# Output projection of a hybrid decoder layer by seven half-size products instead of eight

## The chip, the cores and the metric

The kernel runs on one core of one Trainium2 chip. The metric is the device time of one execution in microseconds (us), as the median of several runs. The engines are called as the profile calls them: PE (TensorE, matrix products; PEld is its weight load), DVE (VectorE), ACT (ScalarE), POOL (GpSimd) and SP (SyncE, which here only issues transfers). Each engine runs its own instructions in a fixed order and waits for the others by semaphores; SP, ACT and POOL each issue transfers in the order of their own instructions.

## What is computed

One decoder layer over 2048 tokens of width 1024, in float32. The change touches the first block's last step, the output projection, and what feeds it:

```python
h = rmsnorm(x, mix_norm_w[i])
proj = h @ w_in[i]
y_s5  = s5_mixer(...)            # diagonal SSM group, 256 columns, ends in y * sigmoid(y @ w_glu)
y_ssd = ssd_mixer(...)           # Mamba-2 group, 768 columns, ends in rmsnorm(y * silu(z), norm_w)
x = x + concatenate([y_s5, y_ssd], -1) @ w_out[i]      # 2048x1024 by 1024x1024
h = rmsnorm(x, xa_norm_w[i])
x = x + cross_attention(h, mem_n, wq, wk, wv, wo)
h = rmsnorm(x, ffn_norm_w[i])
x = x + conv_ffn(h, w_up, conv_w, conv_b, w_down)
return rmsnorm(x, final_norm_w)
```

The rmsnorm inside `ssd_mixer` divides each token's 768 columns by their own root mean square. The 256 columns of `y_s5` are not divided by it.

## The kernel before

Every float32 product is made of three matmuls on split operands: an operand is cut into a rounded high part (ACT, `halves`, L98) and the low rest (DVE, L99), and `mm3` (L123 to L125) adds high by high, high by low and low by high. A matmul has 128 stationary columns and 512 moving ones. So each operand costs one ACT and one DVE instruction per 128x512 tile before PE can take it.

The stages run in this order.

1. **The mixer** (`MixerIn.run`, four blocks of 512 tokens): the input projection, the convolutions, the SSD scan. Its results go to the DRAM tensor `yT`, one 128x1024 row of tiles per 128 tokens, columns 256 to 1023. Generators in the lists `fg`, `bg` and `xg` are advanced a step at a time between the halves of the projections (`Kit.step`). `ssq` makes `rs`, the reciprocal root mean square per token.
2. **The S5 part** (`stage_s5`): its last piece, `glu` (L868 to L876), multiplies gelu by a gate on DVE (L874) and writes columns 0 to 255 of `yT` with a POOL transfer (L875), block by block. Cross-attention's weight products run beside it.
3. **`stage_b`**: the output projection, then the scores, softmax and values of cross-attention. Scores and values already run by seven half-size products (`products`, Strassen-Winograd): two token tiles (a "pair", eight pairs in all) give the four quarters a11, a12, a21, a22 of the left side; `lefts` forms and splits the seven left factors, one per product; `factors` and `right` form and split the seven right factors, 4 tiles of 128x512 per product. `ORDER` (1, 6, 5, 3, 7, 4, 2) is the order of the products.
4. The feed-forward stages `stage_up` and `stage_down`.

In `stage_b` before, the output projection runs tile by tile (16 token tiles, 2 halves of the columns). Per half, `proj` multiplies the six `yT` chunks of the SSD group (p2) and the two of the S5 group (p1) into two PSUM tiles, and DVE adds `rs` * p2 and 0.5 * p1 to x (L1215, L1216). The 16 tiles of `w_out` are split once into the `Q` buffers (7 groups of 8). The first four half-tiles start with the chunks 2, 3, 6 and 7 (`early`), which do not need the S5 part. Towards the end the first right factors of the scores (`Rg`) go into the `Q` groups that are still free, and the left factors of the scores' first pair are made from x1, the result written to DRAM by POOL (L1217).

Raw tiles come through pools: `F` (10 tiles of 128x512), `L` (2 tiles of 128x1024), `X` (6 of 128x1024), `A` (16 left halves). A pool's tile can be loaded again only when its last reader is done.

What stands in which order on an engine is set by the tile scheduler, which orders the program's instructions by priorities and dependences; within an engine nothing overtakes.

## Time and profile before

| what | value |
|---|---|
| time, median of 3 runs | 2668.95 us (2668.3 to 2670.01) |
| time of the profiled execution | 2667.42 us |
| its span | 2665.7 us |
| PE busy | 2603.0 us (98%) |
| DVE busy | 2121.5 us (80%) |
| ACT busy | 1358.0 us (51%) |
| POOL busy | 407.3 us (15%) |
| first and last matmul of `stage_b`'s products | 848.6 and 1367.9 us |
| the output projection, by its first matmul and its last addition to x | 848.6 to 1028.4 us |

Matmuls are pipelined, so the duration of one (389 ns) is longer than the distance between two. The same is true of DVE and ACT instructions: the distance between the starts of two is what a queue costs. Windows and timelines count from the span's start.

### The profile page before, as it was taken

What the parts mean: (1) busy time and instruction counts of PE and PEld (TensorE: products, weight loads), DVE (VectorE), ACT (ScalarE), POOL (GpSimd) and SP (SyncE); (2) the same over time, 40 slices, a digit from 0 to 9 for tenths busy, and PEclk for the clock granted to TensorE, in tenths of its full rate; (3) what the DMA queues carried; (4) which work ended last, traced back from release to release, by engine and by line L of the source; (5) the groups of instructions that cost most, each with busy time, mean ns of one, the idle gap of its engine ahead of it and who ended that gap; (6) DMA issues with size and microseconds to landing.
All of it is one profiled execution on the core that took longest, in us unless ns stands there. A gap on an engine that the chain in (4) does not pass through costs nothing. (4 is left out here: it accounts for less than half of the span.)

```text
span 2665.7 us, 38967 instructions
## 1 busy us (share of the span) xinstructions
PE 2603.0 (98%) x12796; PEld 2150.3 (81%) x12796; DVE 2121.5 (80%) x4034; ACT 1358.0 (51%) x2817; POOL 407.3 (15%) x691
## 2 busy tenths in 40 slices
PE   8999999999999999999999999999999999999998
PEld 6768878788987888888888888888888887788876
DVE  8798898888876537778788878989787877678776
ACT  4655567764556116788554545445444434433333
POOL 1112212111022101202202332212111110000000
PEclk9999999999999999999999999999999999999999
DMA  5565554543586936546762444344222218887886
GB/s 188 173 186 175 182 192 164 164 139 126 177 303 235 336 126 213 182 168 231 261 202 83 128 146 133 103 123 153 80 87 80 87 64 280 278 283 249 262 263 209
DMA packets 244355, 480.94 MB, mean 180 GB/s; under 512 B 30584, under 2 KB 72824, under 8 KB 244152
## 3 DMA queue, kind: packets, MB, share of 16 engines
q1 hardware_dynamic: 182312, 341.38, 38.3%
q0 software_dynamic: 32976, 118.09, 13.8%
q10 hardware_dynamic: 28864, 18.98, 2.3%
q8 instruction: 101, 1.65, 0.3%
q14 instruction: 102, 0.84, 0.1%
HBM read 363.25 MB, written 114.49 MB: 179 GB/s over the span
## 5 line engine op out<-in xcount | busy, mean ns | idle before, releaser
L124 PE MATMUL ps<-H,W 128*128 128x512 f32 x952 | 370.6, 389 | 0.3 <-DVE H L99 0.3
L123 PE MATMUL ps<-H,W 128*128 128x512 f32 x952 | 370.8, 390 | 0.0
L125 PE MATMUL ps<-H,W 128*128 128x512 f32 x952 | 370.4, 389 | 0.0
L123 PE MATMUL ps<-h,w 128*128 128x512 f32 (+1 forms) x736 | 299.1, 406 | 3.1 <-DVE h L102 2.1
L124 PE MATMUL ps<-h,w 128*128 128x512 f32 (+1 forms) x736 | 286.6, 389 | 0.9 <-DVE h L102 0.9
L125 PE MATMUL ps<-h,w 128*128 128x512 f32 (+1 forms) x736 | 286.3, 389 | 0.7 <-DVE w L99 0.7
L123 PE MATMUL ps<-Q,A 128*128 128x512 f32 x704 | 275.8, 392 | 0.8 <-ACT A L98 0.8
L125 PE MATMUL ps<-Q,A 128*128 128x512 f32 x704 | 274.5, 390 | 0.2 <-DVE A L99 0.2
L124 PE MATMUL ps<-Q,A 128*128 128x512 f32 x704 | 273.9, 389 | 0.0
L98 ACT ACTIVATE W<-S 128x512 fp32r<-128x512 f32 x191 | 119.0, 630 | 292.8 <-DVE S L1346 146.1
L98 ACT ACTIVATE w<-r 128x512 fp32r<-128x512 f32 x224 | 139.4, 627 | 139.5 <-PE ps L124 108.7
L124 PEld LDWEIGHTS ps<-H,W 128*128 128x128 f32 x952 | 178.7, 188 | 38.0 <-DVE H L99 1.1
L125 PEld LDWEIGHTS ps<-H,W 128*128 128x128 f32 x952 | 178.7, 188 | 37.2
L123 PEld LDWEIGHTS ps<-H,W 128*128 128x128 f32 x952 | 178.7, 188 | 37.0 <-ACT H L98 0.3
L99 DVE TENSOR_TENSOR w<-r,w 128x512 fp32r<-128x512 f32 x224 | 153.5, 687 | 33.0 <-ACT w L98 31.4
L125 PEld LDWEIGHTS ps<-h,w 128*128 128x128 f32 x736 | 139.4, 189 | 30.6 <-DVE w L99 1.1
L123 PEld LDWEIGHTS ps<-h,w 128*128 128x128 f32 x736 | 139.6, 190 | 29.7 <-DVE h L102 2.3
L124 PEld LDWEIGHTS ps<-h,w 128*128 128x128 f32 x736 | 139.8, 190 | 27.6 <-DVE h L102 2.5
L125 PEld LDWEIGHTS ps<-Q,A 128*128 128x128 f32 x704 | 132.2, 188 | 29.1 <-DVE A L99 1.4
L123 PEld LDWEIGHTS ps<-Q,A 128*128 128x128 f32 x704 | 132.2, 188 | 27.8 <-ACT A L98 1.0
L124 PEld LDWEIGHTS ps<-Q,A 128*128 128x128 f32 x704 | 132.3, 188 | 26.6
L98 ACT ACTIVATE A<-F 128x512 fp32r<-128x512 f32 (+1 forms) x146 | 89.1, 631 | 126.4 <-PE ps L124 74.1
(474 smaller groups left out, 6187.4 us busy)
## 6 DMA issues: line engine op xcount, KB each, us to landing
A<-actd SPq DMA_DIRECT2D x192, 256.0 KB, 3.6
r<-in_w_in SPq DMA_DIRECT2D x176, 256.0 KB, 2.9
R<-in_w_up SPq DMA_DIRECT2D x176, 256.0 KB, 2.8
R<-in_w_down SPq DMA_DIRECT2D x132, 256.0 KB, 4.3
actd<-U POOLq DMA_DIRECT2D x88, 256.0 KB, 3.1
A<-actd SPq DMA_DIRECT2D x96, 192.0 KB, 3.6
R<-h3Cd SPq DMA_DIRECT2D x56, 256.0 KB, 3.2
L<-acsd POOLq DMA_DIRECT2D x32, 384.0 KB, 4.4
```

Of the source, the lines that this page charges most:

```text
L98: self.S.activation(hi, src, AF.Copy)
L99: self.V.tensor_tensor(lo, src, hi.bitcast(F32), op=ALU.subtract)
L123: self.TE.matmul(out, lh, rh, start=first and i == 0, stop=False)
L124: self.TE.matmul(out, lh, rl, start=False, stop=False)
L125: self.TE.matmul(out, ll, rh, start=False, stop=last and i == n - 1)
```

## The change

The output projection now runs by pairs through `products`, like the scores.

- Since one matrix product now has to take both groups of columns, the S5 columns carry half the root mean square of the SSD columns (`iv`) from where they are made: `ssq` makes `iv` and writes it to DRAM, `glu` loads it broadcast over the partitions and multiplies each gate's result by it. The whole product is then scaled by `rs`.
- `out_factors`, a new generator at the end of `bg`, forms four right factors of `w_out` in the mixer (16 loads, 16 DVE additions, 16 POOL writes to `Ot`).
- `stage_b` loads and splits seven right factors (28 tiles of 128x512 instead of 16), each into its own group of `Q` (`qm`), and the left factors of each pair from two `L` tiles that hold the rows of `yT` (`yprep`, `parts`). The first pair runs the products in the order 4, 2, 1, 6, 5, 3, 7; 4 and 2 need the SSD columns only. The results go through `put` into x (L1243, L1245).
- The scores' right factors `Rg` are made in the last pair, one product's group after the other, as each `Q` group comes free.

```diff
@@ ssq
+        iv = self.sp.tile([P, 4], F32, tag="iv", name="iv")
+        k.V.tensor_scalar(iv, pq[:, 0:4], 0.0625 / 768, 0.25e-6, op0=ALU.mult, op1=ALU.add)
         k.rstd(self.d["rs"][:, b * 4:b * 4 + 4], pq[:, 0:4], 0.25 / 768, 1e-6)
+        k.G.tensor_tensor(iv, iv, k.p05[:, 0:1].to_broadcast([P, 4]), op=ALU.pow)
+        k.G.dma_start(out=self.d["iv"][b].rearrange("(c p) -> p c", p=P), in_=iv)
@@ run
+        k.bg.append(out_factors(k, self.a, self.d))
+def out_factors(k, a, d):
+    w, V = a["w_out"], k.V
+    put = lambda i, j, t: k.G.dma_start(out=d["Ot"][i, j], in_=t)
+    for j in range(4):
+        b11, b12 = (k.load(w[j][:, n * 512:n * 512 + 512]) for n in range(2))
+        t1, t2 = k.t(), k.t()
+        V.tensor_tensor(t1, b12, b11, op=ALU.subtract)
+        put(0, j, t1)
+        yield
+        b22 = k.load(w[4 + j][:, 512:1024])
+        V.tensor_tensor(t2, b22, t1, op=ALU.subtract)
+        put(1, j, t2)
+        V.tensor_tensor(b12, b22, b12, op=ALU.subtract)
+        put(2, j, b12)
+        yield
+        b21 = k.load(w[4 + j][:, 0:512])
+        V.tensor_tensor(b21, t2, b21, op=ALU.subtract)
+        put(3, j, b21)
+        yield
+        yield
@@ glu
+            iv = k.t()
+            G.dma_start(out=iv, in_=d["iv"][b].partition_broadcast(P))
                 V.scalar_tensor_tensor(th, th, 1.0, gf[o, b], op0=ALU.add, op1=ALU.mult)
+                V.tensor_tensor(th, th, iv, op=ALU.mult)
                 G.dma_start(out=d["yT"][b * 4:b * 4 + 4, :, o, :].rearrange("c p n -> p c n"), in_=th.rearrange("p (c n) -> p c n", c=4))
@@ stage_b
-    qp = ring(8, qs)
+    early = (4, 2)
+    order0 = early + tuple(m for m in ORDER if m not in early)
+    qm = dict(zip(order0, qs))
@@ right
-            out.append(split(k.load(src, fp()), qp))
+            out.append(split(k.load(src, fp()), qm[m]))
@@ stage_b, the output projection
-    for t in range(NT):
...
-            p2 = proj(act, nh, (4, 5), head[t, nh]) if (t, nh) in head else proj(act, nh, range(2, 8))
-            p1 = proj(act, nh, [0, 1])
-            V.scalar_tensor_tensor(x[:, s], p2, d["rs"][:, t:t + 1], x[:, s], op0=ALU.mult, op1=ALU.add)
-            V.scalar_tensor_tensor(x[:, s], p1, 0.5, x[:, s], op0=ALU.mult, op1=ALU.add)
...
+    def yprep(p):
+        ys = []
+        for t in (2 * p, 2 * p + 1):
+            ys.append(k.load(row(t), xl()))
+        (a11, a12), (a21, a22) = ((y[:, 0:512], y[:, 512:1024]) for y in ys)
+        return parts(a11, a21, a22, a12)
+    Rw, Rg, L = {}, {}, {}
+    with tc.issue_after(after.ins):
+        for m in early:
+            Rw[m] = right("O", m)
+    a11, a21, a22, a12 = ap(), ap(), fp(), fp()
...
+    L[4], L[2] = split(a22, ap), split(a12, ap)
...
+    gen = yprep(1)
+    for p in range(NP):
...
+        def put(i, j, x, y, op):
+            c = tmp() if (i, j) == (1, 1) else x if i else y
+            V.tensor_tensor(c, x, y, op=op)
+            x = xs[i][:, j * 512:j * 512 + 512]
+            V.scalar_tensor_tensor(x, c, d["rs"][:, 2 * p + i:2 * p + i + 1], x, op0=ALU.mult, op1=ALU.add)
+        def after(m):
+            Ln[next(left)] = next(gen)
+            if p + 1 == NP:
+                Rg[m] = right("G", m)
+            if m == 7 and 1 <= p <= 4:
+                factors("G", p - 1)
+        products(k, terms(L, Rw), tmp, put, after, ORDER if p else order0)
...
+        gen, L = yprep(p + 2) if p + 2 < NP else xprep(p + 2 - NP), Ln
```

**Three places in the order of the instructions.** First, DVE where the output projection begins. The names: `Q` are split right factors, `A` split left factors, `F` raw tiles, `t` the S5 part's tiles. Before, the last splits of `w_out` and the two 256-column halves that hold the S5 columns of tiles 0 and 1:

```order
L99 TENSOR_TENSOR Q3_10187<-F_10184,Q3_10186 128x512
L99 TENSOR_TENSOR Q2_10169<-F_10166,Q2_10168 128x512
L99 TENSOR_TENSOR Q3_10193<-F_10190,Q3_10192 128x512
L99 TENSOR_TENSOR A_10125<-F_10122,A_10124 128x256
L99 TENSOR_TENSOR A_10135<-F_10132,A_10134 128x256
L99 TENSOR_TENSOR A_10259<-F_10256,A_10258 128x512
```

Of the change, from the last of the new multiplies in `glu` (L907) to the first left factor that holds S5 columns (A_10297, product 1):

```order
L907 TENSOR_TENSOR t_10135<-t_10135,t_10114 128x512
L101 TENSOR_TENSOR Q2_10249<-F_10246,Q2_10248 128x512
L101 TENSOR_TENSOR Q3_10273<-F_10270,Q3_10272 128x512
L101 TENSOR_TENSOR Q2_10255<-F_10252,Q2_10254 128x512
L101 TENSOR_TENSOR Q3_10279<-F_10276,Q3_10278 128x512
L101 TENSOR_TENSOR Q2_10261<-F_10258,Q2_10260 128x512
L101 TENSOR_TENSOR Q3_10285<-F_10282,Q3_10284 128x512
L101 TENSOR_TENSOR Q2_10267<-F_10264,Q2_10266 128x512
L101 TENSOR_TENSOR Q3_10291<-F_10288,Q3_10290 128x512
L101 TENSOR_TENSOR A_10297<-A_10230,A_10296 128x512
L1179 TENSOR_TENSOR F_10300<-A_10231,F_10232 128x512
```

The left factor of product 1 now stands behind eight splits of right factors, and these behind eight more instructions of `glu`; 25 rows further stands the last split of the seventh right factor (Q6_10391).

Second, DVE where one pair's left factors end and the next pair's begin. `L` are the two raw row tiles, `M` the sums of products, `X` the rows of x. Of the change:

```order
L1245 SCALAR_TENSOR_TENSOR X_10398<-M_10453,rs_95,X_10398 128x512
L101 TENSOR_TENSOR A_10540<-L_10394,A_10539 128x512
L1056 TENSOR_TENSOR M_10585<-ps_10572,M_10566 128x512
L101 TENSOR_TENSOR A_10569<-L_10545,A_10568 128x512
L1059 TENSOR_TENSOR M_10608<-ps_10595,M_10585 128x512
```

Before, the same stage of DVE around one token tile:

```order
L1215 SCALAR_TENSOR_TENSOR X_10441<-ps_10637,rs_91,X_10441 128x512
L99 TENSOR_TENSOR A_10758<-F_10755,A_10757 128x512
L1216 SCALAR_TENSOR_TENSOR X_10441<-ps_10656,X_10441 128x512
L99 TENSOR_TENSOR A_10760<-F_10756,A_10759 128x512
L1215 SCALAR_TENSOR_TENSOR X_10512<-ps_10680,rs_91,X_10512 128x512
```

L_10545 takes the buffer of L_10394, whose last reader is A_10540; A_10569, which needs L_10545, stands two rows behind. From A_10569 to the last left factor made of the same `L` tiles there are 24 rows; in the following pairs 23, 24, 24, 19 and 20.

Third, PE where the last pair begins. `ident` rows are transposes of x1 for the scores' first pair. Of the change:

```order
L125 MATMUL ps_11547<-Q2_10266,A_11395 128x512
L126 MATMUL ps_11547<-Q2_10267,A_11395 128x512
L127 MATMUL ps_11547<-Q2_10266,A_11396 128x512
L150 MATMUL ps_11566<-ident_66,L_11523 128x128 x4
L150 MATMUL ps_11572<-ident_66,L_11533 128x128 x4
```

and SP's transfers ahead of them:

```order
L113 DMA L_11372<-yTd_80 128x1024
L113 DMA L_11374<-yTd_80 128x1024
L1196 DMA L_11523<-x1d_81 128x1024
L1196 DMA L_11533<-x1d_81 128x1024
L1196 DMA L_11886<-x1d_81 128x1024
L113 DMA F_11594<-Gd_77 128x512
```

Before, SP loads these x1 tiles far ahead, between two tiles' rows of `yT`:

```order
L1122 DMA X_10601<-in_x 128x1024
L1177 DMA L_11294<-x1d_79 128x1024
L111 DMA F_10595<-yTd_78 128x512
L111 DMA F_10596<-yTd_78 128x512
L111 DMA F_10666<-yTd_78 128x512
```

The transposes now follow the last pair's product 1 directly, and their tiles take the buffers of L_11372 and L_11374, the last pair's own rows. The loads for `Rg` (F_11594 is the first) stand behind L_11886, which takes the buffer of L_11523. On DVE the 28 splits of `Rg` follow, mixed with the last pair's sums and the left factors of the scores' first pair: from the first of these left factors (A_11591) to the last split of `Rg` (Q1_11881) there are 52 rows, and 13 rows later stands the first left factor of the scores' second pair.

More of the change, by code (lines that the diff above doesn't have):

```diff
@@ L1005, with products, use @@
 ORDER = (1, 6, 5, 3, 7, 4, 2)
-def products(k, terms, tmp, put, after):
-    V, M = k.V, {}
-    for m in ORDER:
-        o = M[m] = k.ps()
-        k.mm3(o, terms(m))
+def products(k, terms, tmp, put, after, order=None):
+    V, M, u = k.V, {}, {}
+    todo = list(ORDER)
+    def use(m):
+        o = M[m]
         if m == 1:
-            m1 = tmp()
-            k.S.activation(m1, o, AF.Copy)
+            u[1] = tmp()
+            k.S.activation(u[1], o, AF.Copy)
         elif m == 6:
-            u2 = tmp()
-            V.tensor_tensor(u2, o, m1, op=ALU.add)
+            u[2] = tmp()
+            V.tensor_tensor(u[2], o, u[1], op=ALU.add)
         elif m == 5:
-            u4 = tmp()
-            V.tensor_tensor(u4, o, u2, op=ALU.add)
+            u[4] = tmp()
+            V.tensor_tensor(u[4], o, u[2], op=ALU.add)
         elif m == 3:
-            put(0, 1, o, u4, ALU.add)
+            put(0, 1, o, u[4], ALU.add)
         elif m == 7:
-            V.tensor_tensor(u2, o, u2, op=ALU.add)
-            put(1, 1, M[5], u2, ALU.add)
+            V.tensor_tensor(u[2], o, u[2], op=ALU.add)
+            put(1, 1, M[5], u[2], ALU.add)
         elif m == 4:
-            put(1, 0, u2, o, ALU.subtract)
+            put(1, 0, u[2], o, ALU.subtract)
         else:
-            put(0, 0, o, m1, ALU.add)
+            put(0, 0, o, u[1], ALU.add)
+    for m in order or ORDER:
+        M[m] = k.ps()
+        k.mm3(M[m], terms(m))
+        while todo and todo[0] in M:
+            use(todo.pop(0))
         after(m)
@@ L1109, in split @@
         return hi, lo
-    W, ys = {}, {}
-    def yprep(t, cuts):
-        y = d["yT"][t].rearrange("p a b -> p (a b)")
-        raw, act = [fp() for _ in range(2)], [(ap(F32R), ap(F32R)) for _ in range(2)]
-        ys[t] = (act, xp())
-        for lo, hi in cuts:
-            hf, s = lo // 512, slice(lo % 512, lo % 512 + hi - lo)
-            k.halves(k.load(y[:, lo:hi], raw[hf][:, s]), act[hf][0][:, s], act[hf][1][:, s])
-            yield
-        nc.sync.dma_start(out=ys[t][1], in_=a["x"][t * 128:t * 128 + 128, :])
-        yield
-    def proj(act, nh, kts, p=None, last=True):
-        first, p = p is None, p or k.ps()
-        terms = []
-        for kt in kts:
-            h, l = act[kt // 4]
-            s = slice((kt % 4) * 128, (kt % 4) * 128 + 128)
-            terms.append((h[:, s], l[:, s], *W[kt][nh]))
-        k.mm3(p, terms, first, last)
-        return p
     def factors(nm, j):
@@ L1157, in lefts, with parts @@
             S.activation(o, k.tr4(x, hf), AF.Copy)
+        yield from parts(a11, a21, a22, a12)
+    def parts(a11, a21, a22, a12):
         yield split(a11, ap)
@@ L1227, in terms @@
         return f
+    row = lambda t: d["yT"][t].rearrange("p a b -> p (a b)")
+    def yprep(p):
[9 more added lines that the diff above has]
+    a11, a21, a22, a12 = ap(), ap(), fp(), fp()
+    for o, t, lo, n in ((a22, 1, 512, 512), (a12, 0, 512, 512), (a11, 0, 256, 256), (a21, 1, 256, 256)):
+        k.load(row(t)[:, lo:lo + n], o[:, lo % 512:lo % 512 + n])
+    L[4], L[2] = split(a22, ap), split(a12, ap)
+    for m in order0[2:4]:
+        Rw[m] = right("O", m)
+    for o, t in ((a11, 0), (a21, 1)):
+        k.load(row(t)[:, 0:256], o[:, 0:256])
+    gen = parts(a11, a21, a22, a12)
+    for m in ORDER[:5]:
+        L[m] = next(gen)
+    for m in order0[4:]:
+        Rw[m] = right("O", m)
+    gen = yprep(1)
+    for p in range(NP):
+        xs, Ln, left = [], {}, iter(ORDER)
+        for t in (2 * p, 2 * p + 1):
+            xs.append(xp())
+            nc.sync.dma_start(out=xs[-1], in_=a["x"][t * 128:t * 128 + 128, :])
+        def put(i, j, x, y, op):
[10 more added lines that the diff above has]
+        products(k, terms(L, Rw), tmp, put, after, ORDER if p else order0)
+        for i in range(2):
+            t = 2 * p + i
+            G.dma_start(out=d["x1"][t * 128:t * 128 + 128, :], in_=xs[i])
+        gen, L = yprep(p + 2) if p + 2 < NP else xprep(p + 2 - NP), Ln
+    ahead = gen
     def small(nm, n):
@@ L1244, in soft @@
         G.dma_start(out=d["p"][t * 128:t * 128 + 128, :], in_=s)
-    ahead = xprep(1)
-    for m in ORDER[1:]:
-        if m not in Rg:
-            Rg[m] = right("G", m)
-        if m not in L:
-            L[m] = next(gen)
     Rv = {}
```

36 lines of the change are left out of this document (3 added, 33 removed).

## The prediction

> **What bounds the kernel now.** I read the page's busy times, then the windows of the stage that changes, then the timelines of PE and DVE at its two ends.
>
> ```profile
> span 2665.7 us, 38967 instructions
> ...
> PE 2603.0 (98%) x12796; PEld 2150.3 (81%) x12796; DVE 2121.5 (80%) x4034; ACT 1358.0 (51%) x2817; POOL 407.3 (15%) x691
> ```
>
> PE is the bound: it is idle for 63 of 2666 us. So work taken from PE is worth its full length if the others keep up. The windows (start and end, length, then busy us and count of PE, PEld, DVE, ACT and POOL, the clock, the DMA share and GB/s) tell how much room they have around the output projection:
>
> ```profile
> 360.00:410.00 50.00, 49.73 (x304) 39.95 (x303) 43.43 (x123) 27.16 (x73) 12.00 (x18) 1.00 0.50 163
> 840.00:860.00 20.00, 20.00 (x86) 15.63 (x85) 18.43 (x32) 17.32 (x34) 6.01 (x8) 0.96 0.78 244
> 860.00:1000.00 140.00, 140.00 (x619) 115.97 (x618) 67.33 (x106) 21.86 (x39) 16.88 (x31) 1.00 0.66 236
> 1000.00:1060.00 60.00, 60.00 (x291) 50.40 (x290) 46.90 (x84) 37.39 (x79) 6.99 (x12) 1.00 0.66 233
> ```
>
> PE waits for nothing from 840 to 1060. DVE has half its time free from 860 to 1000, and almost none in the 20 us before, where the S5 part ends. I use 0.2% of the time, 5.3 us, as what can be told from no change.
>
> **What is removed.** 96 matmuls: 768 (16 tiles x 2 halves x 8 chunks x 3) become 672 (8 pairs x 7 products x 4 chunks x 3). Their price is the distance between two, not the 389 ns of one:
>
> ```profile
> 857.07 0.39 PE L123 MATMUL ps<-Q,A 128*128 128x512 f32 x1
> ...
> 879.51 0.39 PE L123 MATMUL ps<-Q,A 128*128 128x512 f32 x1
> ```
>
> Between these two rows lie 33 groups of three: 22.44 / 99 = 0.2267 us. Gain: 96 x 0.2267 = **21.8 us**. A pair is then 84 matmuls, 19.0 us of PE, and a product 2.72.
>
> **What is added to DVE.** The rows that price it, from DVE's timeline at the end of the S5 part:
>
> ```profile
> 841.59 1.49 DVE L874 SCALAR_TENSOR_TENSOR t<-t 128x512 f32<-128x512 f32 x2
> 843.00 0.68 DVE L99 TENSOR_TENSOR Q<-F,Q 128x512 fp32r<-128x512 f32 x1
> 844.93 0.69 DVE L99 TENSOR_TENSOR t<-t 128x512 fp32r<-128x512 f32 x1 [1.24 <-ACT t L98]
> ...
> 850.96 2.49 DVE L874 SCALAR_TENSOR_TENSOR t<-t 128x512 f32<-128x512 f32 x4
> 853.37 0.68 DVE L99 TENSOR_TENSOR A<-F,A 128x512 fp32r<-128x512 f32 x1
> 853.97 4.29 DVE L99 TENSOR_TENSOR Q<-F,Q 128x512 fp32r<-128x512 f32 x7
> ```
>
> Seven rows in 4.29 us: 0.613 us per row where DVE never waits. I price every added row so.
>
> *Where the projection begins.* Before, DVE is through the last gates at 853.4. Eight multiplies (L907) are added; two fit into the 1.24 us wait, so now it is 853.4 + 8 x 0.613 - 1.2 = 857.1. Then eight splits of right factors, then the split that product 1 needs: 857.1 + 9 x 0.613 = 862.6. Its transfer is not the later one: the gates of block 0 go out at 842.57, their load is issued at 847.73, and the ACT split follows at 853.03; two multiplies later, that is about 855.
>
> ```profile
> 842.57 1.56 POOL L875 DMA_DIRECT2D yTd<-t  x2 [16.84 <-DVE t L874]
> ...
> 847.73 0.33 SPq L111 DMA_DIRECT2D F<-yTd  x1
> ...
> 853.03 0.72 ACT L98 ACTIVATE A<-F 128x256 fp32r<-128x256 f32 x2
> 851.82 0.39 PE L124 MATMUL ps<-Q,A 128*128 128x512 f32 x1
> ```
>
> PE is done with the gates at about 851.8, now 0.6 later; products 4 and 2 have 20 matmuls left (4.5 us), product 1 two before it needs the split: PE stops at 857.4 and waits 5.2. From there DVE leads: 25 rows on, at 877.9, it finishes the seventh right factor, and PE has the first pair and product 1 of the second behind it at 879.6, where without waits it would be at 873.2. **6.4 us lost.** The first pair makes 28 right splits within one pair's time; before, 16 were needed and 48 matmuls could start without the S5 part.
>
> *From pair to pair.* The raw rows sit in two `L` tiles, one pair's worth. DVE's last split of a pair frees them; only then SP loads the next pair's, ACT splits, DVE splits. DVE stands in that wait, since almost nothing else is ahead in its queue. Such loads of 512 KB, from the waits for `L` between 1051 and 1062 and over 885 to 1140:
>
> ```profile
> DMA to landing us min/median/max: 4.2/4.8/5.4
> ...
> DMA to landing us min/median/max: 3.5/6.1/7.5
> ...
> 1034.57 0.63 ACT L1045 ACTIVATE F<-L 128x512 f32<-128x512 f32 x1 [1.54 <-DVE Q L99]
> 1035.11 0.19 ACT L1045 ACTIVATION_READ_ACCUMULATOR F<-L 128x1 f32 x1
> ```
>
> I take 4.5 for the first of two loads, between the lowest and the median of the first line, with 0.3 for the semaphores, 0.63 on ACT and 0.6 on DVE: 6.0 us from a pair's last split to the next pair's first. A round of DVE is then 23 steps x 0.613 + 6.0 = 20.1 us for 24 rows, 19.5 for 23, 17.0 and 17.6 for the last two, against 19.0 on PE. It hardly loses, but never makes up its late start. Walked row by row: first pair's end as above; the second pair's left factors are done at 888.2 (17 rows after 877.9), the third pair's first at 894.2, its second 10 rows later at 900.3, where PE is at 898.5: 1.8 lost; the same once more before the seventh pair, 1.2. **3.0 us lost.** The last pair's first split comes at 991.0, its last 19 rows later at 1002.7; PE ends the seventh pair at 994.0.
>
> *The last pair.* PE has the transposes of x1 right behind the last pair's product 1, and their tiles can only be loaded after that split at 1002.7. Before, these loads were issued long ahead of the transposes:
>
> ```profile
> 887.33 0.32 SPq L1177 DMA_DIRECT2D L<-x1d  x1
> ...
> 899.74 0.57 SPq L1177 DMA_DIRECT2D L<-x1d  x1
> ...
> 1003.28 1.91 PE L148 MATMUL ps<-ident,L 128*128 128x128 f32 x16
> 1003.91 2.07 ACT L1157 ACTIVATE F<-ps 128x512 f32<-128x512 f32 x4 [21.79 <-PE ps L148]
> ```
>
> Both tiles are there 6.1 us later (0.2, and 5.9 for the second load: 0.4 more than the 5.4 above, for its later issue, and 0.1), at 1008.8. PE is through product 1 at 996.7: **12.1 us lost**, the largest term.
>
> *Into the scores.* Four squares (0.63 + 0.19 each), a copy, four copies (2.07) and a split on ACT put DVE's next section at 1014.5. It holds the 28 splits of `Rg`, which before lay spread:
>
> ```profile
> L99 DVE TENSOR_TENSOR Q<-F,Q x28: 676/682/693, 943.8 to 1033.8; 128x512 fp32r<-128x512 f32 x28
> ```
>
> 52 rows later (1046.4) the last is done, and 13 rows on, five of them small, the scores' second pair gets its first left factor at 1052.0. PE, product by product, waits 1.0, 1.6 and 2.9: **5.5 us lost.** Before, nothing waited there.
>
> *In the mixer.* 16 additions on DVE, 16 POOL writes and 16 loads fall into block 1, about 361 to 410, where DVE is busy for 43.4 of 50 us. 16 x 0.613 = 9.8 us do not fit into 6.6 idle, so between 0 (moved into later gaps: S5 set-up work beside it is not urgent) and 9.8 reaches PE; I take **2.0**, nearer to 0 because weights are split a projection ahead. The four `iv` steps are like these two, which make `rs` (from the view of that tile):
>
> ```profile
> L130 DVE TENSOR_SCALAR rs<-ps x4: 151/156/163, 266.9 to 723.6; 128x4 f32<-128x4 f32 x4
> L131 POOL TENSOR_TENSOR rs<-rs,m x4: 1358/1444/1481, 267.3 to 723.8; 128x4 f32<-128x4 f32 x4
> ```
>
> Four times 0.16 us on DVE and 1.4 on POOL, which is busy for 12 of 50 us above; and the last one, at about 724, lies over 100 us ahead of the first gates: nothing. If POOL's writes held up its own loads of decay rows behind them, that would fall under the same bound.
>
> A wait can cost more than its length. Here PE waits 2.66 us, and its clock is at half in the next 8 us, 4 us of work lost:
>
> ```profile
> 526.66 0.49 PE L438 MATMUL ps<-t 128*128 128x128 f32 x2 [2.66 <-DVE t L316]
> ...
> 520.00:528.00 8.00, 4.60 (x23) 3.37 (x23) 6.25 (x14) 6.58 (x17) 0.54 (x1) 0.97 0.37 118
> 528.00:536.00 8.00, 8.00 (x40) 6.56 (x41) 5.05 (x14) 1.71 (x7) 0.54 (x1) 0.50 0.43 141
> ```
>
> I add nothing for it: after each long wait PE runs into DVE's next late row, which hides up to 5.5 us. The Trainium skill (TensorE: Matmul & The Clock Gate, Part 1: The HAM clock gate) has the array fall to half rate after an idle window of about 3.4 us; the row above agrees in the half. By that rule the waits of 5.2 and 12.1 us would each be followed by some 3.4 us at half rate, an estimated 3.4 us more in all if nothing hid it.
>
> **The sum.** -21.8 + 6.4 + 3.0 + 12.1 + 5.5 + 2.0 = **+7.2 us**. Against the profiled span of 2665.7 that is 2672.9; the profiled execution took 2667.4 and the median is 2668.95, so 2676.2, and I say **2676**. DVE, not PE, sets the pace for 190 us.
>
> **Rivals.** *Short refill* (same): with 3.5 us, the lowest row, a round takes 19.1, 18.5 and 16.0 to 16.6 us, DVE catches up, the waits become 6.4 + 0.8 + 7.1 + 5.5, and the mixer hides its part: -2.0, **2667**. For it: that load was almost alone, as these may be. Against: 1 MB of x, 1 MB of x1 and for four pairs 2 MB of factors move in the same rounds. The Trainium skill (DMA: Bandwidth & Descriptors, Anatomy of one DMA) prices a transfer at 2.0 us and its bytes by 436 GB/s, an estimated 3.2 us for 512 KB; with it the sum would be about -3; the rows above are all longer. *DVE keeps up* (faster): if its rows overlap the waits better than the queue order lets me see, only the wait for the first S5 columns (5.2) and one exposed load before the transposes (about 3.5) stay: -21.8 + 8.7 = -13, **2656**. For it: half of DVE is free from 860 to 1000. Against: it starts that stretch late, and the refill gap is idle time nobody can use. *Long refill* (much slower): with 6.1 us rounds take 21.7 and 18.6, the waits become 6.4 + 10.8 + 15.2 + 5.5, and with 6 in the mixer the sum is +22, **2691**; it decides from about 5.3 us on. That the change doesn't do what it says can be left aside: the order has the fewer matmuls.
>
> **How the numbers follow.** Forecast 0.42 (own range 2671 to 2684), long refill 0.17, short refill 0.20, DVE keeps up 0.21. Slower by over 0.2%: 0.40 + 0.17 = 0.57; within: 0.20 + 0.02 = 0.22; faster: 0.21. The range reaches from the faster case to the long refill: 2657 to 2690.
>
> **What would show it.** Right: 96 fewer matmuls; a DVE busy over 80% from 860 to 1010; PE waits for a split `A` or `Q` near 857, none of that before; a wait of 6 to 14 us before the transposes of x1 and, in DVE's row of that stage, idle times that end on a DMA into `L` or on ACT's split of it, 4 to 7 us, once per pair. Wrong: PE busy without gaps from 860 to 1060 and the later stages 10 us or more earlier than before; or the loss not here but in the mixer, with the projection's first matmul already late by more than 4 us.

## The result, and the profile after

The changed kernel takes 2702.43 us (median; 2697.91 to 2707.04) beside 2668.95 before: a ratio of 1.0125, interval 1.0111 to 1.014. It is slower by about 33 us, where the prediction said 2676 with a range up to 2690. The sign was right, the size was not.

The page of the changed kernel:

```profile
span 2701.2 us, 39006 instructions
...
PE 2600.8 (96%) x12700; PEld 2141.7 (79%) x12700; DVE 2188.5 (81%) x4153; ACT 1379.5 (51%) x2859; POOL 426.7 (16%) x719
```

PE has its 96 matmuls fewer, but is busy for 2.2 us less, not 21.8, and idle for 100 us instead of 63. Its mean granted clock fell from 0.994 to 0.986, and a matmul takes longer at a lower clock (0.63 us instead of 0.39 from 893 to 895, where the clock was 0.50). Three long windows show where; first of before, then of the changed kernel (length, busy us and count of PE, PEld, DVE, ACT, POOL, the clock, DMA share, GB/s):

```profile
200.00:742.00 542.00, 531.96 (x3173) 439.37 (x3172) 467.76 (x1042) 329.68 (x768) 91.41 (x129) 0.99 0.52 169
742.00:865.00 123.00, 115.69 (x716) 102.11 (x715) 90.11 (x158) 75.37 (x173) 30.02 (x66) 0.99 0.77 259
865.00:1080.00 215.00, 215.00 (x983) 179.01 (x982) 128.05 (x215) 72.66 (x155) 27.68 (x50) 1.00 0.64 228
```

```profile
200.00:742.00 542.00, 519.22 (x3042) 424.34 (x3042) 469.73 (x1047) 321.32 (x753) 102.75 (x145) 0.98 0.55 173
742.00:865.00 123.00, 111.27 (x755) 101.70 (x754) 78.63 (x140) 64.64 (x153) 31.14 (x68) 0.97 0.82 261
865.00:1080.00 215.00, 192.22 (x819) 155.46 (x818) 176.82 (x295) 88.96 (x174) 28.73 (x49) 0.94 0.71 244
```

PE's idle time grows from 10.0 to 22.8 us in the mixer, from 7.3 to 11.7 around the S5 part, and from 0 to 22.8 in the output projection, where its clock falls too. To tell the stages apart I use three marks that every kernel has: the last `rs` (end of the mixer), the last POOL write of `yT` (end of the S5 part) and the last transpose of a left factor of scores or values. Before (the row of `rs` stands in the prediction), and in the changed kernel:

```profile
L875 POOL DMA_DIRECT2D yTd<-t x8: 750/750/772, 842.6 to 856.5; - x8
...
L148 PE MATMUL ps<-ident,L x256: 270/272/331, 1003.3 to 1332.6; 128*128 128x128 f32 x128
```

```profile
L132 DVE TENSOR_SCALAR rs<-ps x4: 150/154/155, 269.9 to 742.1; 128x4 f32<-128x4 f32 x4
...
L908 POOL DMA_DIRECT2D yTd<-t x8: 750/757/775, 869.9 to 887.7; - x8
...
L150 PE MATMUL ps<-ident,L x256: 270/273/447, 1033.6 to 1368.4; 128*128 128x128 f32 x128
```

The mixer ends 18.5 us later (742.1 for 723.6). The S5 part takes 145.6 us instead of 132.9, the stretch from there to the last transpose 480.7 instead of 476.1: together +35.8, and the rest of the layer is as long as before (1332.8 and 1333.1 us). So 31 of the 36 us are lost by the last `yT` write, where the prediction had put 2.0 for the mixer and 3.7 for the multiplies. PE's longest waits, from its timeline:

```profile
396.49 0.42 PE L367 MATMUL ps<-da,tri 128*128 128x48 f32 x2 [2.53 <-DVE da L362]
...
462.62 0.48 PE L431 MATMUL ps<-ident,t 128*128 128x128 f32 x1 [6.47 <-DVE t L318]
...
887.93 0.80 PE L126 MATMUL ps<-Q,A 128*128 128x512 f32 x1 [3.79 <-DVE Q L101]
892.75 0.80 PE L127 MATMUL ps<-Q,A 128*128 128x512 f32 x1 [4.02 <-DVE A L101]
...
1033.61 1.08 PE L150 MATMUL ps<-ident,L 128*128 128x128 f32 x4 [5.49 <-DMA L<-x1d]
1036.38 2.79 PE L150 MATMUL ps<-ident,L 128*128 128x128 f32 x12 [1.68 <-DMA L<-x1d]
...
1075.43 0.79 PE L125 MATMUL ps<-Q,A 128*128 128x512 f32 x1 [4.16 <-DVE M L1056]
```

The last five rows are the head, the last pair and the step into the scores, all foretold. The wait of 6.47 us at 462 was not. The rows of POOL, ACT and DVE just before it lead to its cause:

```profile
446.97 0.81 POOL L516 DMA_DIRECT2D ivd<-iv  x1 [0.29 <-POOL iv L515]
...
450.35 0.60 POOL L797 DMA_DIRECT2D tabd<-tab  x1 [1.32 <-DVE t L309]
...
459.92 0.22 ACT L788 ACTIVATE tab<-fb 128x16 f32<-128x16 f32 x1 [7.09 <-DMA tabd<-tab]
...
460.75 0.35 DVE L794 SCALAR_TENSOR_TENSOR tab<-tab,Er,w 128x128 f32<-128x128 f32 x1 [6.34 <-ACT w L793]
```

POOL stores `iv`, then a finished S5 table. ACT needs that table's buffer and waits 7.1 us for its write to land; DVE waits for ACT, and PE for DVE. The landing times in the DMA view (median us to landing last), for a window of 1 us ahead of the store of `iv` (443 to 444), one around it, and one around the table's write at 450:

```profile
r<-in_w_in SPq DMA_DIRECT2D x1, 256.0 KB, 2.6
tabd<-tab POOLq DMA_DIRECT2D x1, 256.0 KB, 2.6
...
r<-in_w_in SPq DMA_DIRECT2D x1, 256.0 KB, 9.5
ivd<-iv POOLq DMA_DIRECT2D x1, 2.0 KB, 9.8
...
tabd<-tab POOLq DMA_DIRECT2D x1, 256.0 KB, 9.6
```

The 2 KB of `iv` take 9.8 us (the four stores 9.8 to 10.4), and a 256 KB transfer that is under way with them takes 9.5 instead of 2.6, on SP's queue as on POOL's. The store writes 512 pieces of 4 bytes (token c * 128 + p lies in partition p, column c). The Trainium skill (DMA: Bandwidth & Descriptors, Specifications) gives 512 bytes as the least transfer for the full rate; read as the size of a piece, these rows agree that 4 bytes are slow, but e1's pieces of 16 bytes are below it too and land in 2.5 us. Its fit of 2.0 us plus bytes (Anatomy of one DMA) would give an estimated 2.0 us for 2 KB, and the measured 9.8 decides. Whether it is the pieces that count is what e1 tests.

### The profile page after: what moved, and what is told of

Read it like the earlier page. It is cut to its first block, busy times and chain, and to the rows that moved or that the text cites. A ratio compares the mean times of both kernels' runs of the same rounds, so it can differ in the third digit from the quotient of the medians.

```text
span 2701.2 us, 39006 instructions
## 1 busy us (share of the span) xinstructions
PE 2600.8 (96%) x12700; PEld 2141.7 (79%) x12700; DVE 2188.5 (81%) x4153; ACT 1379.5 (51%) x2859; POOL 426.7 (16%) x719
## 5 line engine op out<-in xcount | busy, mean ns | idle before, releaser
L125 PE MATMUL ps<-Q,A 128*128 128x512 f32 x672 | 265.5, 396 | 6.7 <-DVE M L1056 4.2
L127 PE MATMUL ps<-Q,A 128*128 128x512 f32 x672 | 264.2, 393 | 4.4 <-DVE A L101 4.4
L126 PE MATMUL ps<-Q,A 128*128 128x512 f32 x672 | 263.6, 392 | 3.8 <-DVE Q L101 3.8
L100 ACT ACTIVATE w<-r 128x512 fp32r<-128x512 f32 x224 | 139.3, 627 | 150.7 <-PE ps L126 115.9
L125 PEld LDWEIGHTS ps<-Q,A 128*128 128x128 f32 x672 | 127.6, 190 | 33.9 <-DVE M L1056 4.6
L127 PEld LDWEIGHTS ps<-Q,A 128*128 128x128 f32 x672 | 127.3, 189 | 33.7 <-DVE A L101 7.0
L126 PEld LDWEIGHTS ps<-Q,A 128*128 128x128 f32 x672 | 127.5, 190 | 30.2 <-DVE Q L101 4.2
L315 DVE SCALAR_TENSOR_TENSOR t<-t,cw 128x512 f32<-128x512 f32 x168 | 128.5, 765 | 12.8 <-ACT t L313 12.0
```

Source lines behind the costliest of these rows:

```text
L100: self.S.activation(hi, src, AF.Copy)
L125: self.TE.matmul(out, lh, rh, start=first and i == 0, stop=False)
L126: self.TE.matmul(out, lh, rl, start=False, stop=False)
L127: self.TE.matmul(out, ll, rh, start=False, stop=last and i == n - 1)
L315: k.V.scalar_tensor_tensor(xc, gb[:, q:q + 512], cw[:, j, q:q + 1], xc, op0=ALU.mult, op1=ALU.add)
```

## The experiments

The marks in the profiled execution of each kernel, in us, and its ratio to the kernel before, timed beside it, with the interval. Two columns are differences of marks. What follows the last mark is the same code everywhere and took 1332.8 to 1342.6 us, so a single execution wanders by up to 10 us there. The marks wander less, but they do where the code is the same: the last `rs` by 4 us in four kernels with the changed mixer (changed, e4, e6, e8), and by 5.7 between e15 and e16. Each row is one execution.

| kernel | last rs | to last yT write | to last transpose | ratio |
|---|---|---|---|---|
| before | 723.6 | 132.9 | 476.1 | 1 |
| changed | 742.1 | 145.6 | 480.7 | 1.0125 (1.0111 to 1.0140) |
| e1 iv in 16-byte pieces | 731.0 | 147.0 | 480.3 | 1.0109 (1.0087 to 1.0131) |
| e2 no factors made | 728.4 | 144.1 | 482.0 | 1.0087 (1.0066 to 1.0109) |
| e3 no iv | 730.6 | 132.1 | 482.2 | 1.0044 (1.0029 to 1.0060) |
| e4 four L tiles | 742.1 | 144.9 | 466.2 | 1.0084 (1.0058 to 1.0110) |
| e5 e1, iv loaded early | 731.7 | 141.5 | 482.3 | 1.0092 (1.0071 to 1.0113) |
| e6 as changed | 740.1 | 147.0 | 482.1 | 1.0129 (1.0108 to 1.0151) |
| e7 first full version | 732.6 | 139.3 | 471.4 | 1.0037 (1.0023 to 1.0052) |
| e8 spare matmuls | 738.1 | 145.7 | 479.5 | 1.0136 (1.0115 to 1.0157) |
| e9 factors a block later | 732.8 | 149.2 | 479.7 | 1.0120 (1.0104 to 1.0135) |
| e10 e5, POOL multiplies | 735.8 | 146.8 | 479.5 | 1.0114 (1.0097 to 1.0130) |
| e11 second full version | 728.7 | 146.9 | 470.1 | 1.0049 (1.0033 to 1.0064) |
| e12 third full version | 730.1 | 137.3 | 481.8 | 1.0062 (1.0048 to 1.0077) |
| e13 e1 and e2 | 724.0 | 146.6 | 483.8 | 1.0080 (1.0061 to 1.0099) |
| e14 S5 part of e12 alone | 734.7 | 137.5 | 494.1 | 1.0120 (1.0100 to 1.0140) |
| e15 fourth full version | 726.9 | 144.5 | 470.9 | 1.0037 (1.0025 to 1.0049) |
| e16 e15, other order | 732.6 | 140.2 | 471.6 | 1.0031 (1.0018 to 1.0044) |

### The mixer: iv's store or the factors

**e1**, another layout of `iv` in DRAM:

```diff
-        k.G.dma_start(out=self.d["iv"][b].rearrange("(c p) -> p c", p=P), in_=iv)
+        k.G.dma_start(out=self.d["iv"][b].rearrange("(p c) -> p c", p=P), in_=iv)
@@ glu
-                V.tensor_tensor(th, th, iv, op=ALU.mult)
+                V.tensor_tensor(th.rearrange("p (c n) -> p c n", c=4), th.rearrange("p (c n) -> p c n", c=4), iv.rearrange("p (n c) -> p c n", c=4), op=ALU.mult)
```

> Same result, only another layout of iv in DRAM: each partition writes its four values side by side, 128 pieces of 16 bytes instead of 512 pieces of 4 bytes; the multiply in glu reads them with a stride. Theory Q (queue): in the changed kernel the 2 KB of iv take about 10 us to land on POOL's queue, the tab writes behind them are late, ACT, DVE and PE wait 6 to 7 us in block 1, the clock falls after that wait, and the S5 tables are late after block 3. Then the store lands in under 4 us, the 6.5 us wait at 462 is gone and the time is 2684 to 2693. Theory T (traffic: the 16 loads, adds and writes of the factors slow the mixer, and iv's store only happens to lie there): 2699 to 2703.

**e2**, no factors: the line `k.bg.append(out_factors(...))` is gone, and `right` reads four quarters of `w_out` in their place, so the output is not the layer's.

> Leaves the making of four right factors out (16 loads, 16 additions, 16 POOL writes in the mixer); the products 5, 6, 7 and 4 take raw quarters of w_out instead, so the output is not the layer's. Theory T (traffic): the mixer's loss of 18 us is mostly theirs, time 2684 to 2692, and the first matmul of block 2's SSD part comes at nearly the time of before. Theory Q: what they cost is the waits at 371, 396 and 436 (1.2 + 2.5 + 2.2 us) and some slow clock, 2694 to 2698; iv's wait of about 6 us stays in the trace.

**e3**, no `iv`: its lines in `ssq` and `glu` are gone, so the S5 columns are not scaled.

> Leaves iv out altogether (its two steps and its store in ssq, its load and the eight multiplies in glu), so the S5 columns are not scaled. Theory Q: all that the narrower store gains, and beside it the head of the projection: 8 multiplies (4.9 us of DVE), 4.1 us in which DVE waits for the loads of iv, so some 7 us less waiting of PE where the products begin: 2676 to 2686. Theory T: only the head, 2692 to 2697.

**e13**, the edits of e1 and e2 together.

> The 16-byte layout and no making of the four factors (their products take raw quarters, so the output is not the layer's). The mixer's loss of 15 to 18 us is 4.8 with iv alone and 7.0 with the factors alone. If iv's loss there is the 10 us for which its 512 pieces hold POOL's queue, the last rs comes within 2 us of before's 723.6; if it is iv's instructions on DVE and POOL, 3 to 5 us stay. The S5 part keeps its 11 to 14 us in either case, since glu's loads and multiplies are untouched: ratio 1.006 to 1.009.

In e1 the store lands in 2.5 us (the four of them in 2.1 to 5.9), as its DMA view has it for the time around that store:

```profile
tabd<-tab POOLq DMA_DIRECT2D x1, 256.0 KB, 3.1
ivd<-iv POOLq DMA_DIRECT2D x1, 2.0 KB, 2.5
```

The wait at 462 is gone and the mixer ends at 731.0, 11 us earlier than in the changed kernel. By the ratio the gain is smaller: 1.0109, 2696 us, which is in the range of neither theory (Q 2684 to 2693, T 2699 to 2703), and the interval overlaps the changed kernel's. e2 (2690.85) falls into theory T's range, e3 (2680.1) into theory Q's. The mixer by itself is clearer: four kernels carry the changed one, and five carry it with the 16-byte store. Each cell has the last `rs` and then PE's idle time from the span's start up to it, as means where there are several:

| last rs; PE idle until then | no factors | factors made |
|---|---|---|
| no iv | 723.6; 28.8 (before) | 730.6; 35.3 (e3) |
| iv in 16-byte pieces | 724.0; 30.2 (e13) | 733.2; 35.8 (e1, e5, e7, e10, e14: 731.0 to 735.8; 34.7 to 38.2) |
| iv in 4-byte pieces | 728.4; 31.3 (e2) | 740.6; 41.3 (changed, e4, e6, e8: 738.1 to 742.1; 40.5 to 42.1) |

The idle time wanders less than the mark. What else the marks show is busy time, 693.9 to 701.0 us for nearly the same matmuls; no run tests what the lower clock costs in the mixer. By the idle time the factors alone cost 6.5 us (7.0 by the marks), the 16-byte store 1.4 (0.4) and the 4-byte store 2.6 (4.8). Factors and 4-byte store together cost 12.5 (17.0), 3 to 5 us more than the two apart (three of the cells behind this are single executions). Beside the factors `iv` costs 6.0 us of idle time with its 4-byte store and 0.5 with the other: so nearly all of its loss in the changed mixer is the store, and its instructions in `ssq` cost little, as foretold.

The long wait of PE needs both. It is 6.47, 5.03, 5.11 and 6.71 us in the four kernels that make the factors just before a 4-byte store. Where this store stands without the factors ahead of it, ACT waits for a table's write too, but for 4.35 and 4.22 us, and PE's wait is shorter. First e2, then e9 (below):

```profile
448.82 0.49 PE L440 MATMUL ps<-t 128*128 128x128 f32 x2 [2.45 <-DVE t L318]
```

```profile
447.49 0.49 PE L440 MATMUL ps<-t 128*128 128x128 f32 x2 [2.50 <-DVE t L318]
```

Theory Q had said that in e2 about 6 us of this wait would stay. Theory Q and theory T each have a part, and neither explains the mixer by itself. Whether the factors cost by their additions on DVE or by their 32 transfers is not separated by any run.

**e6 and e9** move the factors to a later place in the mixer. The edit of e6 is this, and e9 has `self.NB - 1` for the 2:

```diff
-        k.bg.append(out_factors(k, self.a, self.d))
         for b in range(self.NB):
+            if b == 2:
+                k.bg.append(out_factors(k, self.a, self.d))
```

> Only the place of the four factors' making: appended in the mixer's third block instead of the first, where the DMA share is 0.36 to 0.44 and DVE has 6 to 9 us of 50 free. If they cost by crowding transfers and DVE in block 1, the waits at 371, 396 and 436 are gone and nothing takes their place: ratio 1.008 to 1.010, as without the factors. If the 16 additions and transfers cost wherever they stand, 1.011 to 1.014.

> The changed kernel with the factors' generator appended in the mixer's fourth block: its four steps per column then really stand later, between about 500 and 690, spread between other work. If the factors cost by crowding DVE and the transfers of the third block, the waits at 371, 396 and 436 (together 5.9 us) go and the end of the mixer (last rs) comes 8 to 14 us sooner than the changed kernel's 742, ratio 1.007 to 1.010. If they cost wherever they stand, the waits come back at the new place, last rs 738 to 742 and ratio 1.011 to 1.014.

e6 moved nothing: the generator is reached in the third block anyway, their place in DVE's order is the same, and the writes to `Ot` stand at 363 to 420 (366 to 423 in the changed kernel). (The prediction called this block 1, counting wrongly; its times were right.) So e6 is a second measurement of the changed kernel, and agrees: 1.0129. In e9 the waits at 371, 396 and 436 are gone and that at 462 has shrunk, but waits of 0.9 to 1.7 us come at 483, 563, 627 and 668; the mixer ends 9 us earlier than in the changed kernel, the S5 part is the longest of all, and the ratio is 1.0120. A later place gains nothing that can be told in the time.

### The refill of L

**e4**:

```diff
-    ... ("L", 2, 1024), ("X", 6, 1024) ...
+    ... ("L", 4, 1024), ("X", 4, 1024) ...
```

> Four L tiles instead of two, and four X tiles instead of six to make room. If the refill of L is what the last pair costs: the 7.2 us before the transposes of x1 go, with the half clock after them (about 3 us), and DVE loses its idle 13 us over the pairs, so the wait of 4.2 us at the scores' first pair shrinks too: 2686 to 2692. If DVE sets the pace in this stage whatever the refill does, the wait moves to the scores: 2697 to 2702. If four X tiles are too few, PE waits for x in the pairs and it is slower than 2702.

The mixer and the S5 part stand as in the changed kernel, and the products' stretch falls from 480.7 to 466.2, 9.9 below before. PE goes through the transposes of x1 without a wait, and only 2.1 us are left at the scores (the groups of PE's waits from 895 to 1062 in e4):

```profile
PE ps L125 <- DVE M L1056: 2.1, 1, 2.1
```

The ratio, 1.0084, agrees with the refill as the cause: 11 us, of 14.5 by the marks. In this stretch the projection by seven products does gain.

### The S5 part: iv's loads and multiplies

Without `iv` (e3) the S5 part takes 132.1 us; with `iv` loaded and multiplied in `glu` it takes 144 to 149. With the 16-byte store, whose multiplies are slower (below), it stays at 147 (e1, e13): the loads and multiplies are enough to lengthen it, and what the 4-byte store adds here is not shown. In the changed kernel DVE's timeline at its tail reads:

```profile
876.42 1.29 DVE L907 TENSOR_TENSOR t<-t 128x512 f32<-128x512 f32 x2 [1.36 <-DMA t<-ivd]
...
879.44 2.49 DVE L906 SCALAR_TENSOR_TENSOR t<-t 128x512 f32<-128x512 f32 x4
884.23 1.29 DVE L907 TENSOR_TENSOR t<-t 128x512 f32<-128x512 f32 x2 [2.30 <-DMA t<-ivd]
885.98 1.29 DVE L907 TENSOR_TENSOR t<-t 128x512 f32<-128x512 f32 x2 [0.46 <-DMA t<-ivd]
887.20 4.89 DVE L101 TENSOR_TENSOR Q<-F,Q 128x512 fp32r<-128x512 f32 x8
892.01 0.68 DVE L101 TENSOR_TENSOR A<-A 128x512 fp32r<-128x512 f32 x1
```

DVE waits for loads of `iv`: they stand in POOL's queue behind the `yT` writes of the block before, which wait for the multiply of that block. After the last gate come the eight right splits, then the left split that product 1 needs.

**e5**: e1, and the four loads ahead of the S5 loop, into four tiles of their own (issued from 730.7 to 741.5).

```diff
+        vp, ivs = cx.enter_context(k.tc.tile_pool(name="s5iv", bufs=4)), []
+            if g == 2:
+                for b in range(4):
+                    ivs.append(vp.tile([P, 512], F32, tag="iv5", name="iv5"))
+                    G.dma_start(out=ivs[b], in_=d["iv"][b].partition_broadcast(P))
@@ glu
-            iv = k.t()
-            G.dma_start(out=iv, in_=d["iv"][b].partition_broadcast(P))
+            iv = ivs[b]
```

> The 16-byte layout of iv as before, and iv's four loads issued early in the S5 part into four tiles of their own, so that glu only multiplies. Theory Q: in the changed kernel each block's load of iv stands in POOL's queue behind the writes of the block before, which wait for the multiply, which waits for its load: a chain of four loads of 4 to 10 us at the tail. With it gone the last gate comes about 12 us sooner than in the changed kernel with the 16-byte layout, DVE has no wait for iv, PE's two waits of about 4 us at the first pair shrink to 2 to 4 in all: ratio to before 1.004 to 1.007 (2677 to 2686 beside a before of 2667). If the eight multiplies themselves are what is late, no more than 2 us are gained over the 16-byte layout (ratio 1.009 to 1.011).

**e10**: e5, and POOL multiplies gelu by `iv` in place, instead of DVE in `glu`:

```diff
@@ glu
-                V.tensor_tensor(th.rearrange("p (c n) -> p c n", c=4), th.rearrange("p (c n) -> p c n", c=4), iv.rearrange("p (n c) -> p c n", c=4), op=ALU.mult)
...
                 gs[b] = [k.split(gf[i, b]) for i in range(2)]
+                for i in range(2):
+                    gv = gf[i, b].rearrange("p (c n) -> p c n", c=4)
+                    G.tensor_tensor(gv, gv, ivs[b].rearrange("p (n c) -> p c n", c=4), op=ALU.mult)
```

> The run with iv in 16-byte pieces and loaded early, and now POOL multiplies gelu by iv in place, behind the split that reads it, so DVE has none of the eight multiplies. If these multiplies stand on the path at the tail of the S5 part, the stretch from the first gate matmul to the last yT write shrinks from 22.7 us by 4 to 6, and the ratio falls by 0.002 to 0.003 to about 1.006. If POOL is too slow or too late (each gate would wait for it), the stretch grows and the ratio is above 1.010.

e5 shortens the S5 part by 5.5 against e1, to 141.5, and the first pair's two waits become one of 4.45 us; half of the 12 us that theory Q had said, and the ratio, 1.0092, shows little of it. The 16-byte layout has a price of its own: read with a stride, the multiply takes 1.09 us instead of 0.69 (that line in e5, then in the changed kernel):

```profile
L906 DVE TENSOR_TENSOR t<-t,iv x8: 1050/1090/1109, 856.7 to 871.8; 128x512 f32<-128x512 f32 x8
```

```profile
L907 DVE TENSOR_TENSOR t<-t x8: 681/686/694, 868.9 to 886.6; 128x512 f32<-128x512 f32 x8
```

e10 went the other way: 146.8, 1.0114. POOL needs 1.9 us for one multiply, and DVE's split beside it takes 2.0 instead of 0.69. The timelines of both in e10:

```profile
856.38 1.94 POOL L938 TENSOR_TENSOR t<-t,iv 128x512 f32<-128x512 f32 x1 [11.67 <-DVE t L101]
...
856.22 0.69 DVE L101 TENSOR_TENSOR Q<-F,Q 128x512 fp32r<-128x512 f32 x1
856.82 2.06 DVE L101 TENSOR_TENSOR t<-t 128x512 fp32r<-128x512 f32 x1
858.80 0.68 DVE L101 TENSOR_TENSOR Q<-F,Q 128x512 fp32r<-128x512 f32 x1
```

The Trainium skill (SBUF — State Buffer, Who interferes with whom) says that a DVE instruction with two inputs in SBUF and a GpSimd instruction that reads SBUF lock each other out; these rows agree: DVE's row ends 0.56 us after POOL's.

**e14**: e1's store, loads of `iv` in the middle of the S5 part, four dense copies on ACT, and half of the multiplies ahead of the tail:

```diff
+            if g == 4:
+                for b in range(4):
+                    raw = k.t()
+                    G.dma_start(out=raw, in_=d["iv"][b].partition_broadcast(P))
+                    ivs.append(vp.tile([P, 512], F32, tag="iv5", name="iv5"))
+                    S.activation(ivs[b].rearrange("p (c n) -> p c n", c=4), raw.rearrange("p (n c) -> p c n", c=4), AF.Copy)
...
                     yield from fin(0, jh)
+                    for b in (jh * 2, jh * 2 + 1):
+                        gx[b] = xq.tile([P, 512], F32, tag="gx", name="gx")
+                        V.tensor_tensor(gx[b], gf[0, b], ivs[b], op=ALU.mult)
+                        yield
@@ glu
-            iv = k.t()
-            G.dma_start(out=iv, in_=d["iv"][b].partition_broadcast(P))
...
-                V.scalar_tensor_tensor(th, th, 1.0, gf[o, b], op0=ALU.add, op1=ALU.mult)
-                V.tensor_tensor(th, th, iv, op=ALU.mult)
+                V.scalar_tensor_tensor(th, th, 1.0, gf[o, b] if o else gx[b], op0=ALU.add, op1=ALU.mult)
+                if o:
+                    V.tensor_tensor(th, th, ivs[b], op=ALU.mult)
```

> The changed kernel with the 16-byte store and the S5 part of the full version: loads of iv in the middle, dense copies on ACT, half of the multiplies ahead of the tail. Against the run with early loads and a strided read (stretch from last rs to last yT write 141.5 us, 132.9 before, 132.1 without iv): 134 to 138 if the strided multiplies at the tail (1.05 us each) are what is left, 140 or more if it is the loads on POOL's queue. Ratio 1.006 to 1.009.

The S5 part shrinks to 137.5, inside what was expected and 4 us below e5, so the multiplies at the tail are part of what was left; e14 makes them dense and moves four of them forward at once, and so does not tell which of the two helps. But the kernel is no faster: PE waits 13.06 us for the first left split. The added tiles lie in pools of their own, and the loads of eight right factors' tiles are issued only from 870.25 on, when the S5 part is nearly over. That they wait for memory under the new tiles is my reading; e15, which puts these elsewhere, agrees.

### Waits and the clock

**e8** (`fill` is 1 in the first pair and nothing in the others):

```diff
+        if fill == m:
+            lh, ll, rh, rl = terms(4)[0]
+            for _ in range(32):
+                k.TE.matmul(M[m], lh, rh, start=True, stop=True)
         k.mm3(M[m], terms(m))
@@ after(m), last pair, m = 1
+                for _ in range(32):
+                    k.TE.matmul(spare, lh, rh, start=True, stop=True)
```

> The changed kernel with 32 matmuls more (7.3 us) on PE ahead of the first pair's product 1 and 32 ahead of the transposes of x1, on operands that are there, into a tile that is overwritten or never read: they fill the waits with work that serves nothing. If the clock that falls after a wait costs time, the clock in the windows behind (0.81, 0.68 and 0.66 in the changed kernel) stays near 1.0, and the kernel with more work is not slower, by up to 5 us faster: ratio 1.009 to 1.013. If the low clock costs nothing, the ratio is 1.0125 to 1.014.

Three slices of the changed kernel after its waits, and the same of e8:

```profile
880.00:890.00 10.00, 4.94 (x20) 3.39 (x18) 7.24 (x13) 4.29 (x9) 3.01 (x4) 0.81 0.82 233
890.00:900.00 10.00, 7.25 (x24) 5.88 (x25) 9.78 (x17) 5.02 (x10) 0.00 (x0) 0.68 0.97 347
1030.00:1040.00 10.00, 4.71 (x19) 4.19 (x20) 4.96 (x11) 5.07 (x13) 2.21 (x4) 0.66 0.63 219
```

```profile
880.00:890.00 10.00, 8.68 (x39) 6.87 (x38) 9.14 (x15) 0.36 (x1) 3.01 (x4) 1.00 0.79 271
890.00:900.00 10.00, 9.46 (x39) 6.77 (x38) 9.80 (x17) 8.88 (x17) 0.00 (x0) 1.00 0.94 321
1030.00:1040.00 10.00, 10.00 (x54) 8.53 (x53) 4.48 (x10) 6.16 (x13) 1.68 (x3) 1.00 0.81 267
```

The clock stays at 1.00 with PE kept busy, and 64 matmuls more (14.5 us) cost nothing in the stretch (479.5 for 480.7). But nothing is gained either: the ratio, 1.0136, is in the range expected if the low clock costs nothing, though its interval (from 1.0115) reaches into the other range too, and the wait into the scores is the same 4.1 us. So the slow work in this stretch is real, but what PE saves of it it waits for DVE a little later.

### All mends together

e7 has e5 and e4 (and the move of e6, which does nothing). e11 adds e9 and e10. e12 has e4, e9, e14 and another order of the first pair's splits:

```diff
-    for m in order0[2:4]:
-        Rw[m] = right("O", m)
+    Rw[1] = right("O", 1)
+    r6 = list(raws("O", 6))
...
     for m in ORDER[:5]:
         L[m] = next(gen)
+        if m == 1:
+            Rw[6] = [split(r, qm[6]) for r in r6]
```

e15 is e12 without this order, and with `iv` and the multiplied gelu in tiles that the S5 part has free (`big()` for `vp.tile` and `xq.tile`). e16 is e15 with the order of e12.

> All mends together: iv in 16-byte pieces and loaded early, the factors made in the third block, four L and four X tiles. If the losses add up as the single runs show them (iv about 8 by store and chain beside 5 for the multiplies, factors 10, L 11 us), some 35 us come off the changed kernel: ratio 0.996 to 1.002. If they hide behind one another, 1.003 or more.

> All mends: iv in 16-byte pieces, loaded early, multiplied on POOL; factors in the fourth block; four L and four X tiles. By the single runs' anchors the mixer keeps 0 to 4 us of its 18.5, the S5 part 0 to 3 of its 12.7, and the product stage gains 5 to 10 where the changed kernel lost 4.6: 2666 to 2657 beside a before of 2667, ratio 0.996 to 1.000. Above 1.003 the losses hide behind one another.

> iv in 16-byte pieces, loaded in the middle of the S5 part and laid out densely there by four ACT copies; the first half of gelu multiplied by it there too, so only four multiplies stay at the tail; factors in the fourth block; four L and four X tiles; in the first pair the four splits for product 6 stand behind the left split of product 1. By the anchors: end of the mixer +3 to +6 us against before, S5 part 0 to +4, product stage -6 to -11: ratio 0.997 to 1.002. If DVE's tail of the S5 part and the late splits cannot be shortened this way (all waits only move), 1.003 to 1.006 as in the two versions before.

> The full version again, with iv and the multiplied gelu in tiles that the S5 part has free, not in pools of their own (in the run before these lay over memory of the raw right factors' pool, so their loads were issued only after the last gate and PE waited 12.7 us for the first left split), and without the other order of the first pair's splits. Mixer +3 to +6 us against before, S5 part 0 to +4, product stage -6 to -11 by the anchors: ratio 0.997 to 1.002. 1.003 or more if the waits only move.

> As e15, with the four splits for product 6 behind the left split of product 1. If PE's wait of about 4.4 us at the first left split is the eight right splits ahead of it, it shrinks by 2.4: 2 us faster than e15. If it is the load of the S5 columns, the same as e15.

None beats the kernel before. e7, e15 and e16 come to 1.003 to 1.004, so some 24 of the 33 us are accounted for and given back. In e11 the POOL multiplies keep the S5 part at 146.9. e12 failed as e14 did, by a wait of 12.7 us at the first left split; with the tiles elsewhere (e15) it is 1.25. e15 and e16 cannot be told apart, since the wait of 4.4 us that e16 was to halve is 1.25 in both. What is left in e15, by the marks: 3.3 us in the mixer and 11.6 in the S5 part, against 5.2 gained in the products. e16 has the same source up to there and shows 9.0 and 7.3: the two parts together (14.9 and 16.3) agree, their shares do not. e15's waits around the S5 part are spread (the groups of PE's waits from 742 to 880):

```profile
PE ps L859 <- DMA t<-wwd: 3.9, 3, 2.8
PE ps L879 <- DVE t L866: 3.5, 3, 2.2
PE ps L859 <- ACT b L924: 2.0, 1, 2.0
```

Which of the added instructions makes these S5 tables late is open; only leaving `iv` out (e3) brought that part back to its old length.

## Why the prediction was wrong, step by step

- **Removed, 21.8 us**: right, 96 matmuls fewer.
- **The head, 6.4**: 7.8 (3.79 + 4.02), and for the reason given: eight right splits, then the left one. That DVE comes there 33.8 us later than before (887.2 for 853.4) and not 3.7 belongs to the points on the mixer and on `iv` below.
- **From pair to pair, 3.0**: 2.1 (0.63, 1.14 and 0.34). DVE's waits there, in the changed kernel from 895 to 1040:

```profile
DVE A L101 <- ACT A L100: 9.5, 8, 3.3
DVE F L1179 <- DMA L<-yTd: 7.0, 4, 2.3
...
DVE F L1179 <- DMA x1d<-X: 2.2, 1, 2.2
```

  With 3.6 for factors of the scores, which are no refill, that is 22.3 us: at most 3.2 for each of seven refills, not 6.0, since DVE had additions to x to do in between.
- **The last pair, 12.1**: 7.2, since DVE came there less late; e4 shows that the refill is the cause. **Into the scores, 5.5**: 4.2, and e4 halves it.
- **The clock, nothing**: the three slices above alone hold 4.9 us of slow work (busy time by what the clock lacks of 1). e8 shows that the decision to price it at nothing was nearly right for the end time of this stretch; for the mixer nothing tests it. The Trainium skill's rule on idle windows (TensorE: Matmul & The Clock Gate, Part 1: The HAM clock gate), with which I had estimated 3.4 us more, shows in the clock and not in the end time: the clock fell behind waits of 3.8 to 5.5 us. But the prediction's own row has it at half behind a wait of 2.66 us, shorter than the rule's 3.4.
- In all, the stretch from the last `yT` write grew by 4.6 us. The sum without the mixer's term had said 5.2 for this stretch and the S5 part together, of which 3.7 (the later last multiply) fall into the S5 part; the two grew by 17.3. For the stretch alone that leaves 1.5. It was right in kind: the four waits came to 21.3 us (7.8, 2.1, 7.2 and 4.2) instead of 27.0, and slow work that had been put at nothing came beside them. That the stretch ends near the 5.2 says nothing for the sum.
- **The mixer, 2.0**: this step failed; it measured 14.5 to 18.5 in four executions, of which 12.5 are idle time of PE. The bound had been the DVE time of 16 additions, 0 to 9.8, and the factors alone did cost 7.0 (e3): I took too low a value inside a fair bound. The sentence that POOL's writes, if they held up its own loads, would fall under the same bound was too narrow: `iv`'s store held up transfers of POOL's and SP's queues, and factors and store together went beyond 9.8.
- **"The four `iv` steps ... nothing"**: this is the second and larger failure. I priced the instructions that issue (0.16 and 1.4 us, which cost little, e13) and not the store's pieces. The store of 512 pieces holds up what is under way with it for 9.8 us. The sentence that the last one lies 100 us ahead of the first gates looked at who needs `iv`, not at what stands behind it. And the four loads were not walked in POOL's queue at all: with the multiplies they make the S5 part 13 us longer (e3), where I had 3.7 for the multiplies.
- **Rivals**: none was this one. The long refill gave 2691 with 6 in the mixer; it came nearest in the total and was wrong in the place, since the refill was short. One of the signs named in advance did show it: the loss "in the mixer, with the projection's first matmul already late" (876.0 instead of 848.6).

## What to carry to other kernels

Price a transfer by the number of its pieces and by what else is under way, not by its bytes: here 512 pieces of 4 bytes took 9.8 us, where 256 KB took 2.6, and others paid it. Ask of every small step that is added to an in-order queue what stands behind it, not only who needs its result. And a saving on the busiest engine is worth only what its suppliers can follow: here seven products gained 10 us instead of 21.8 once the refill was mended (e4), and lost 5 before.
